# Differential attention scores: two 128-row passes a map replaced by three 64-row passes, both maps packed on the row halves

## The chip, the core and the metric

The kernel runs on one core of one Trainium2 chip. A core has five engines with instruction streams of their own: TensorE (PE: matmuls, with its weight loads shown apart as PEld), VectorE (DVE), ScalarE (ACT), GpSimd (POOL) and SyncE (SP, which here issues DMAs). Matmuls read SBUF, 128 partitions ("rows") wide, and write PSUM. The metric is the device time of the whole program in microseconds, as a median of several runs.

## The reference

One decoder layer on 1024 tokens of width 1024: RMSNorm, one input projection, an SSD (Mamba-2) mixer and a differential-attention mixer side by side, an output projection, and a SwiGLU feed-forward layer. The part that matters here is the attention, with 8 heads, each with two maps of head dimension 64 and one value of width 128:

```
q = q.reshape(bsz, seqlen, DA_HEADS, 2, DA_HEAD_DIM).transpose(3, 0, 2, 1, 4) * (DA_HEAD_DIM ** -0.5)
k = k.reshape(bsz, seqlen, DA_HEADS, 2, DA_HEAD_DIM).transpose(3, 0, 2, 1, 4)
...
s = jnp.einsum("mbhqd,mbhkd->mbhqk", qi, k).astype(f32)
p = jax.nn.softmax(jnp.where(mask, s, -jnp.inf), axis=-1)
w = p[0] - lam * p[1]
return jnp.einsum("bhqk,bhkv->bhqv", w.astype(v.dtype), v)
```

Each score is a sum over only 64 products. The mask is causal, and the queries go in 8 blocks of 128.

## The kernel before

Wide products are made in float32r. A float32 operand is split into a rounded part ("hi") and the rest ("lo", a second float32r number); `mm3` (L126 to L129) then forms hi·hi + hi·lo + lo·hi in three matmuls that sum up in one PSUM tile. Projections, output projection and feed-forward layer all use it. Values times weights (L611) and the transposes (L607, L624) are plain float32.

For a head, `qk` projects k and q of that head, each as 128 columns (64 of map 0, 64 of map 1) by 1024 tokens in two halves of 512. So the projected PSUM tile has map 0 on rows 0 to 63 and map 1 on rows 64 to 127. Its sinks (`sink_k`, L552 and L553; `sink_q`, L562 to L566) then lay out the operands of the scores so that a 128-row matmul covers two of the 64-product sums at once:

- `KS[:, m]` has the hi part of map m's keys on the map's own 64 rows and the lo part on the other 64 rows.
- `QH[:, m]` has the hi part of the queries on both halves of the rows, `QL[:, m]` the lo part on both.

Every instruction in these sinks works on 64 rows. ACT makes the hi parts (two instructions for k, two for q) and the second copy of QH (two); DVE makes the lo parts (two and two) and the second copy of QL (two).

`att_front(h, i)` makes the scores of head h and query block i. For map m it takes a two-bank PSUM tile `s` (pool `SC`, two buffers), and for each stretch `c` of up to 512 keys it runs two matmuls: QH against KS gives hi·hi + hi·lo (L585), QL against KS gives lo·hi + lo·lo (L586). Then DVE adds the mask (L587) and takes the row maximum (L588), ACT exponentiates and sums (L590), and DVE joins the two maps (L593 to L596). `att_back` of a block runs one step later: transposes (L607), a copy by ACT (L608), and the product with the values (L611). Block i has (i+1)·128 keys, so the score matmuls are 128, 256, 384 or 512 columns wide.

The program's order on each engine is not written out by hand in this stage: a scheduler builds it ahead of time from its own estimate of when operands and buffers are ready, and each engine then runs its list strictly in that order. In the attention it puts the matmuls of the next projections (`mm_q`, `mm_k`, `mm_v`) and of the output projection (`po_s`, `po_a`, L127 to L129) between the short steps of the attention, so that PE has work while DVE and ACT make the softmax. Only the feed-forward part has a PE order by hand.

Of the kernel before, what the change touches and what calls it, by code (L numbers as in the profile page):

```python
# [9 lines left out]
F32 = mybir.dt.float32  # L10
F32R = mybir.dt.float32r
AF = mybir.ActivationFunctionType
ALU = mybir.AluOpType
# [4 lines left out]
P = 128  # L18
# [6 lines left out]
def tile_hybrid_block(  # L25
# [68 lines left out]
    def norm_rows(parts, wbc, outs, name, pool=(), junk=None):  # L94
        """outs = RMSNorm of the row whose column pieces are parts; pieces in pool are weighted on Pool and scaled on ACT"""
        n, w = len(parts), DM // len(parts)
        ss = small.tile([P, n], F32, tag="ss1", name="ss_" + name)
        for i, p in enumerate(parts):
            nc.scalar.activation(outs[i] if junk is None else junk, p, AF.Square, accum_out=ss[:, i:i + 1])
        if n > 1:  # L100
            s1 = small.tile([P, 1], F32, tag="ss1", name="st_" + name)
            nc.vector.tensor_tensor(s1, ss[:, 0:1], ss[:, 1:2], op=ALU.add)
            ss = s1
        r = rstd_of(ss, DM, name)
        for i, (p, o) in enumerate(zip(parts, outs)):
            wi = wbc[:, i * w:i * w + w]
            if i in pool:
                nc.gpsimd.tensor_tensor(o, p, wi, op=ALU.mult)
                nc.scalar.mul(o, o, r)
            else:  # L110
                nc.vector.scalar_tensor_tensor(o, p, r, wi, op0=ALU.mult, op1=ALU.mult)
# [34 lines left out]
    def A4(shape, dt, name):  # L146
        return a4.tile(shape, dt, tag="a4", name=name)
# [15 lines left out]

# [1 line left out]
    def load_raw(src, shape, name):  # L165
# [14 lines left out]
    def z0_raw(a, u):  # L180
        """columns of dt and of the gate of group 0: 264 of 528"""
        raw = wp.tile([P, 4, 264], F32, tag="raw", bufs=2, name=f"wr_z0_{a}_{u}")
        k = slice(4 * u, 4 * u + 4)
        if a == 0:
            nc.sync.dma_start(raw[:, :, 0:16], w_in_k[:, k, C_DT:C_DT + 16])
            nc.sync.dma_start(raw[:, :, 16:264], w_in_k[:, k, C_Z:C_Z + 248])
        else:
            nc.sync.dma_start(raw, w_in_k[:, k, C_Z + 248:C_Z + 512])
        return raw
# [6 lines left out]

# [1 line left out]
    xs = []  # L198
# [16 lines left out]

# [1 line left out]
    prow = P4([69, P], F32, "prow")  # L217
# [17 lines left out]

# [1 line left out]
    def w_unit(src, shape, name, alloc=None):  # L237
# [10 lines left out]
    def proj_T(*jobs):  # L248
        """each job: a weight, a column, a name and sink(half, psum [128 columns, 512 tokens])"""
        us = [w_unit(w_k[:, :, col:col + P], [P, KD, P], name) for w_k, col, name, _ in jobs]  # L250
        for half in range(2):
            for (hi, lo), (_, _, name, sink) in zip(us, jobs):
                ps = MM([P, 512], f"mm_{name}_{half}")
                for k in range(KD):
                    mm3(ps, hi[:, k, :], lo[:, k, :], nhi[half][:, k, :], nlo[half][:, k, :], k == 0, k == KD - 1)
                sink(half, ps)

    def proj_z0(us, name, sink):
        """units of 264 columns; sink(t, psum [128 tokens, 264])"""
        for t in range(NT):  # L260
# [8 lines left out]
    def proj_nat(col, name, sink):  # L269
        """256 columns; sink(t, psum [128 tokens, 2 blocks from t, 256])"""  # L270
        us = [w_unit(w_in_k[:, 4 * u:4 * u + 4, col:col + 256], [P, 4, 256], f"{name}_{u}") for u in range(2)]
# [9 lines left out]

# [1 line left out]
    W16 = [P, NT, 16]  # L283
# [49 lines left out]

# [1 line left out]
    def conv_tiles(*tiles):  # L335
# [21 lines left out]
    def gate_dt():  # L357
        """the gate of group 0 and dt"""
        for a in range(2):
# [151 lines left out]

# [1 line left out]
    cneg = sp.tile([P, P], F32, tag="cs", name="cneg")  # L513
# [13 lines left out]
    def v_pair(hh):  # L527
        # [head][block] views of the two heads; in the last pair but one, the heads' tiles are freed one by one
        by_head = hh == NH // 2 - 2
# [13 lines left out]
    def qk(h):  # L543
        KS, QH, QL = [], [], []
        own = (slice(0, 64), slice(64, 128))

        def sink_k(half, ps):
            ks = A4([P, 2, 512], F32R, f"KS{h}_{half}")
            KS.append(ks)
            for m in range(2):  # L550
                a, b = own[m], own[1 - m]
                nc.scalar.copy(ks[a, m, :], ps[a, :])  # L552
                nc.vector.tensor_tensor(ks[b, m, :], ps[a, :], ks[a, m, :].bitcast(F32), op=ALU.subtract)  # L553

        def sink_q(half, ps):
            qh = A4([P, 2, 512], F32R, f"QH{h}_{half}")
            ql = (CV if h == NH - 1 and half == 0 else A4)([P, 2, 512], F32R, f"QL{h}_{half}")
            QH.append(qh)
            QL.append(ql)
            for m in range(2):  # L560
                a, b = own[m], own[1 - m]
                nc.scalar.mul(qh[a, m, :], ps[a, :], 0.125)  # L562
                nc.vector.scalar_tensor_tensor(ql[a, m, :], ps[a, :], 0.125, qh[a, m, :].bitcast(F32),
                                               op0=ALU.mult, op1=ALU.subtract)
                nc.scalar.copy(qh[b, m, :], qh[a, m, :].bitcast(F32))
                nc.vector.tensor_copy(ql[b, m, :], ql[a, m, :].bitcast(F32))  # L566
        jobs = ((w_in_k, C_K + h * P, f"k{h}", sink_k), (w_in_k, C_Q + h * P, f"q{h}", sink_q))
        for js in ([jobs] if h == NH - 1 else [[j] for j in jobs]):
            proj_T(*js)
        return KS, QH, QL  # L570

    def att_front(h, i, KS, QH, QL):
        n = f"{h}_{i}"
        Lk = (i + 1) * P
        qs = slice(i * P, (i + 1) * P)
        pm = []
        nmx = small.tile([P, 2], F32, tag="nmx", name="nmx" + n)
        sm = small.tile([P, 2], F32, tag="sm", name="sm" + n)
        for m in range(2):
            s = SC([P, T], f"s{n}_{m}")  # L580
            qr = slice((i % 4) * P, (i % 4) * P + P)
            for c in range(i // 4 + 1):
                w = min(Lk - c * 512, 512)
                sc = s[:, c * 512:c * 512 + w]
                nc.tensor.matmul(sc, QH[i // 4][:, m, qr], KS[c][:, m, :w], start=True, stop=False)  # L585
                nc.tensor.matmul(sc, QL[i // 4][:, m, qr], KS[c][:, m, :w], start=False, stop=True)  # L586
            nc.vector.tensor_tensor(s[:, qs], s[:, qs], cneg, op=ALU.add)  # L587
# [71 lines left out]

# [1 line left out]
    KG = 4  # L661
# [14 lines left out]
    def out_block(t, kys, ws, name, bank=MM):  # L676
        """two token blocks from t, 256 columns"""
        ps = bank([P, 2, 256], f"po_{name}_{t}")
# [47 lines left out]

# [1 line left out]
    # gate and up by Winograd's seven products: A are two column tiles by two halves of the contraction, B the two  # L728
    # halves of the contraction by two halves of the tokens; C = A B is summed up in PSUM (X, Y and Z)
    ORDER = (1, 2, 6, 5, 7, 3, 4)  # L730
# [4 lines left out]
    def room(p, early):  # L735
        """an operand B: [hi or lo][block of 128 rows] views of 512 tokens"""
        if early:
# [59 lines left out]
    def ffn_pair(pr, raws, order=ALL, ybank=SC):  # L797
        """silu(gate) * up of two column tiles; they and their sums as operands of the down projection to g_d"""
        sg, tm, c22, reg, sm = {}, {}, {}, [{}, {}], [{}, {}]
# [145 lines left out]
    def final_half(t, nh, last):  # L945
        """the first half of a row to be ready is weighted before its scale is known"""
        ho = h_parts(ho_all, t)
# [12 lines left out]

    # down, by the same seven products: A are the two halves of the tokens by two row tiles, B the row tiles by two
    # halves of the columns
    SLOT = {2: 0, 4: 1, 1: 2, 7: 3, 5: 4, 6: 5, 3: 6}
# [28 lines left out]
    for gi, prs in enumerate(groups):  # L992
# [5 lines left out]
        def psums(two, name):  # L998
            """four banks: one for each block of 128 tokens of a half"""
            if two:  # L1000
# [81 lines left out]
```

## Time and profile before

| | |
|---|---|
| runs, us | 1639.54, 1641.82, 1644.53 (median 1641.82) |
| profiled execution, span, us | 1643.3 (1.5 above the median of the runs) |
| granted TensorE clock | 0.995 |
| PE busy | 1597.2 us, 97%, 9170 matmuls |
| DVE, ACT, POOL busy | 1071.6 us, 775.8 us, 429.2 us |
| attention (first score matmul to the last blocks) | about 387 to 855 us |

The profiled execution's own time is its span; what lies outside it is not in the page. In the profile a matmul's duration runs from its start to a modelled end, and matmuls overlap in the array: the rate at which PE works is read from the distance between starts (about 0.23 us for 512 columns), not from the duration (about 0.39 us). A busy PE row is therefore no proof that PE is at its limit, and distances between starts are looked at beside it.

### The profile page before, as it was taken

What the parts mean: (1) busy time and instruction counts of PE and PEld (TensorE: products, weight loads), DVE (VectorE), ACT (ScalarE), POOL (GpSimd) and SP (SyncE); (2) the same over time, 40 slices, a digit from 0 to 9 for tenths busy, and PEclk for the clock granted to TensorE, in tenths of its full rate; (3) what the DMA queues carried; (4) which work ended last, traced back from release to release, by engine and by line L of the source; (5) the groups of instructions that cost most, each with busy time, mean ns of one, the idle gap of its engine ahead of it and who ended that gap; (6) DMA issues with size and microseconds to landing.
All of it is one profiled execution on the core that took longest, in us unless ns stands there. A gap on an engine that the chain in (4) does not pass through costs nothing. (4 is left out here: it accounts for less than half of the span.)

```text
span 1643.3 us, 23716 instructions
## 1 busy us (share of the span) xinstructions
PE 1597.2 (97%) x9170; PEld 1386.9 (84%) x9170; DVE 1071.6 (65%) x1682; ACT 775.8 (47%) x1608; POOL 429.2 (26%) x378
## 2 busy tenths in 40 slices
PE   6999999999999999999999998999999999999997
PEld 6988878887989989889999987888888888778885
DVE  5345745688776676677674477455555555898987
ACT  6444764456555565575552245333333333334445
POOL 4100330032000000013300034444444443542322
PEclk9999999999999999999999999999999999999999
DMA  5321451143011110147523221233333323944122
GB/s 195 110 79 52 129 163 56 36 142 92 24 46 39 46 33 27 45 130 229 162 77 116 84 99 56 96 102 104 111 116 118 98 96 134 365 166 186 39 103 103
DMA packets 105291, 172.78 MB, mean 105 GB/s; under 512 B 7813, under 2 KB 75530, under 8 KB 103770
## 3 DMA queue, kind: packets, MB, share of 16 engines
q1 hardware_dynamic: 95210, 137.11, 25.2%
q0 software_dynamic: 9968, 34.15, 6.3%
q8 instruction: 72, 1.18, 0.3%
q14 instruction: 41, 0.34, 0.1%
HBM read 125.82 MB, written 45.42 MB: 104 GB/s over the span
## 5 line engine op out<-in xcount | busy, mean ns | idle before, releaser
L127 PE MATMUL x<-n,wa 128*128 128x512 f32 x352 | 138.7, 396 | 0.0
L128 PE MATMUL x<-n,wa 128*128 128x512 f32 x352 | 138.7, 394 | 0.0
L129 PE MATMUL x<-n,wa 128*128 128x512 f32 x352 | 137.8, 394 | 0.0
L590 ACT ACTIVATE p<-s,nmx 128x256 f32<-128x256 f32 (+7 forms) x128 | 94.4, 740 | 53.2 <-DVE nmx L588 49.9
L172 ACT CAST wa<-s 128x512 fp32r<-128x512 f32 x88 | 54.7, 622 | 132.3 <-PE x L129 59.4
L173 DVE TENSOR_TENSOR wa<-s,wa 128x512 fp32r<-128x512 f32 x88 | 76.8, 873 | 51.1 <-ACT wa L172 50.8
L172 ACT CAST dg<-gd 128x512 fp32r<-128x512 f32 x77 | 47.7, 620 | 114.7 <-PE dx L129 57.2
L588 DVE TENSOR_REDUCE nmx<-s 128x1 f32<-128x256 f32 (+7 forms) x128 | 95.3, 754 | 2.4
L173 DVE TENSOR_TENSOR dg<-gd,dg 128x512 fp32r<-128x512 f32 x77 | 66.2, 862 | 23.3 <-ACT dg L172 23.2
L129 PEld LDWEIGHTS x<-n,wa 128*128 128x128 f32 x352 | 66.5, 189 | 15.1
L128 PEld LDWEIGHTS x<-n,wa 128*128 128x128 f32 x352 | 66.6, 189 | 14.8
L127 PEld LDWEIGHTS x<-n,wa 128*128 128x128 f32 x352 | 66.6, 189 | 14.8
L127 PE MATMUL mm_z<-wh_z,nhi 128*128 128x264 f32 (+1 forms) x256 | 75.9, 298 | 2.3 <-ACT wh_z L172 2.3
L611 PE MATMUL o<-v,p 128*128 128x128 f32 x576 | 77.7, 275 | 0.0
L129 PE MATMUL mm_z<-wh_z,nlo 128*128 128x264 f32 (+1 forms) x256 | 77.3, 303 | 0.0
L611 PEld LDWEIGHTS o<-v,p 128*128 128x128 f32 x576 | 73.5, 191 | 2.7
L128 PE MATMUL mm_z<-wl_z,nhi 128*128 128x264 f32 (+1 forms) x256 | 75.0, 294 | 0.0
L127 PE MATMUL mm_v<-wh_v,nhi 128*128 128x256 f32 x256 | 74.2, 290 | 0.0
L129 PE MATMUL mm_v<-wh_v,nlo 128*128 128x256 f32 x256 | 74.1, 290 | 0.0
L128 PE MATMUL mm_v<-wl_v,nhi 128*128 128x256 f32 x256 | 73.5, 287 | 0.0
L128 PE MATMUL po_a<-wl_wo,yh 128*128 128x256 f32 x256 | 72.6, 283 | 0.0
L91 POOL TENSOR_TENSOR rs_o<-ms_o,mhalf 128x4 f32<-128x4 f32 x16 | 18.0, 1125 | 208.4 <-DVE ms_o L89 208.3
(331 smaller groups left out, 5172.9 us busy)
## 6 DMA issues: line engine op xcount, KB each, us to landing
gd<-g_d SPq DMA_DIRECT2D x11, 1792.0 KB, 7.8
wr_g<-in_w_gate_dram SPq DMA_DIRECT2D x22, 512.0 KB, 3.8
wr_u<-in_w_up_dram SPq DMA_DIRECT2D x22, 512.0 KB, 4.3
g_d<-sg SPq DMA_DIRECT2D x22, 512.0 KB, 5.1
wr_d<-in_w_down_dram SPq DMA_DIRECT2D x22, 512.0 KB, 5.0
L<-cs_d POOLq DMA_DIRECT2D x16, 512.0 KB, 4.4
wr_y<-yT_d SPq DMA_DIRECT2D x16, 512.0 KB, 3.8
wr_wo<-in_w_out_dram SPq DMA_DIRECT2D x16, 512.0 KB, 3.5
```

Of the source, the lines that this page charges most:

```text
L91: nc.gpsimd.tensor_tensor(r, ms, mhalf[:, :w], op=ALU.pow)
L127: nc.tensor.matmul(ps, lh, rh, start=first, stop=False, skip_group_check=more)
L128: nc.tensor.matmul(ps, lh, rl, start=False, stop=False, skip_group_check=more)
L129: nc.tensor.matmul(ps, ll, rh, start=False, stop=last, skip_group_check=more)
L172: nc.scalar.copy(hi, raw)
L173: nc.vector.tensor_tensor(lo, raw, hi.bitcast(F32), op=ALU.subtract)
L588: nc.vector.reduce_max(nmx[:, m:m + 1], s[:, :Lk], axis=AX.X, negate=True)
L590: nc.scalar.activation(p[:, :Lk], s[:, :Lk], AF.Exp, bias=nmx[:, m:m + 1], accum_out=sm[:, m:m + 1])
L611: nc.tensor.matmul(o, wT[:, j * P:(j + 1) * P], vt[h % 2][j], start=(j == 0), stop=(j == i))
```

## The change

`KS` now has, on all 128 rows, the hi parts of both maps in slot 0 and the lo parts in slot 1; `QS` likewise for the queries. Each map keeps its own half of the rows, as it comes from the projection. So a sink is one ACT instruction and one DVE instruction on 128 rows in place of two and two (k) or four and four (q), and the tiles `QH` and `QL` become one tile `QS`.

For each stretch of keys and each map, `att_front` now runs three matmuls on 64 rows: hi·hi, hi·lo, lo·hi. lo·lo, which the 128-row form had in passing, is no longer computed. Map 0 uses rows 0 to 63, map 1 rows 64 to 127, and they write different PSUM tiles. The source names them in turn (map 0, map 1, map 0, ...), with both PSUM tiles taken ahead of the first matmul. The rest of the diff removes comments and docstrings.

```
     def qk(h):
-        KS, QH, QL = [], [], []
-        own = (slice(0, 64), slice(64, 128))
+        KS, QS = [], []
         def sink_k(half, ps):
             ks = A4([P, 2, 512], F32R, f"KS{h}_{half}")
             KS.append(ks)
-            for m in range(2):
-                a, b = own[m], own[1 - m]
-                nc.scalar.copy(ks[a, m, :], ps[a, :])
-                nc.vector.tensor_tensor(ks[b, m, :], ps[a, :], ks[a, m, :].bitcast(F32), op=ALU.subtract)
+            nc.scalar.copy(ks[:, 0, :], ps)
+            nc.vector.tensor_tensor(ks[:, 1, :], ps, ks[:, 0, :].bitcast(F32), op=ALU.subtract)
         def sink_q(half, ps):
-            qh = A4([P, 2, 512], F32R, f"QH{h}_{half}")
-            ql = (CV if h == NH - 1 and half == 0 else A4)([P, 2, 512], F32R, f"QL{h}_{half}")
-            QH.append(qh)
-            QL.append(ql)
-            for m in range(2):
-                a, b = own[m], own[1 - m]
-                nc.scalar.mul(qh[a, m, :], ps[a, :], 0.125)
-                nc.vector.scalar_tensor_tensor(ql[a, m, :], ps[a, :], 0.125, qh[a, m, :].bitcast(F32),
-                                               op0=ALU.mult, op1=ALU.subtract)
-                nc.scalar.copy(qh[b, m, :], qh[a, m, :].bitcast(F32))
-                nc.vector.tensor_copy(ql[b, m, :], ql[a, m, :].bitcast(F32))
+            qs = A4([P, 2, 512], F32R, f"QS{h}_{half}")
+            QS.append(qs)
+            nc.scalar.mul(qs[:, 0, :], ps, 0.125)
+            nc.vector.scalar_tensor_tensor(qs[:, 1, :], ps, 0.125, qs[:, 0, :].bitcast(F32),
+                                           op0=ALU.mult, op1=ALU.subtract)
...
-        for m in range(2):
-            s = SC([P, T], f"s{n}_{m}")
-            qr = slice((i % 4) * P, (i % 4) * P + P)
-            for c in range(i // 4 + 1):
-                w = min(Lk - c * 512, 512)
-                sc = s[:, c * 512:c * 512 + w]
-                nc.tensor.matmul(sc, QH[i // 4][:, m, qr], KS[c][:, m, :w], start=True, stop=False)
-                nc.tensor.matmul(sc, QL[i // 4][:, m, qr], KS[c][:, m, :w], start=False, stop=True)
+        ss = [SC([P, T], f"s{n}_{m}") for m in range(2)]
+        for c in range(i // 4 + 1):
+            w = min(Lk - c * 512, 512)
+            for j, (a, b) in enumerate(((0, 0), (0, 1), (1, 0))):
+                for m in range(2):
+                    o = slice(64 * m, 64 * m + 64)
+                    nc.tensor.matmul(ss[m][:, c * 512:c * 512 + w], QS[i // 4][o, a, qr], KS[c][o, b, :w],
+                                     start=j == 0, stop=j == 2)
+        for m, s in enumerate(ss):
             nc.vector.tensor_tensor(s[:, qs], s[:, qs], cneg, op=ALU.add)
```

The scheduler builds a new order for the whole attention. Three places show what it makes of the scores and the sinks. In the names, `s1_6_0` is the score tile of head 1, block 6, map 0; the number after the last underscore belongs to the buffer; `128x384` is the output, and `x3` means three such matmuls in a row.

PE, head 0, block 2 (384 keys), before:

```order
L129 MATMUL mm_q1_0_3821<-nhi0_134,wl_q1_3818 128x512
L585 MATMUL s0_2_0_3504<-KS0_0_3340,QH0_0_3406 128x384
L586 MATMUL s0_2_0_3504<-KS0_0_3340,QL0_0_3407 128x384
L585 MATMUL s0_2_1_3511<-KS0_0_3340,QH0_0_3406 128x384
L586 MATMUL s0_2_1_3511<-KS0_0_3340,QL0_0_3407 128x384
L127 MATMUL mm_q1_1_3856<-nhi1_135,wh_q1_3817 128x512
```

The same scores in the changed program, with the projection's matmuls between the two maps left out here but for the first and the last:

```order
L601 MATMUL wtp0_0_0_3481<-ident_69,p0_0_0_3445 128x128
L578 MATMUL s0_2_0_3490<-KS0_0_3340,QS0_0_3402 128x384 x3
L128 MATMUL mm_q1_1_3851<-nlo1_137,wh_q1_3819 128x512
...
L128 MATMUL mm_q1_1_3851<-nlo1_137,wh_q1_3819 128x512
L578 MATMUL s0_2_1_3491<-KS0_0_3340,QS0_0_3402 128x384 x3
L129 MATMUL mm_q1_1_3851<-nhi1_135,wl_q1_3820 128x512
```

The three 64-row matmuls of one map stand together, and thirteen 128-row matmuls of the projection stand between the maps.

PE, head 1, block 6 (512 and 384 keys), in the changed program:

```order
L605 MATMUL o0_4_4123<-v0_0_3095,p0_4_1_4058 128x128 x4
L578 MATMUL s1_6_0_4133<-KS1_0_3786,QS1_1_3876 128x512 x2
L578 MATMUL s1_6_1_4134<-KS1_0_3786,QS1_1_3876 128x512 x2
L578 MATMUL s1_6_0_4133<-KS1_0_3786,QS1_1_3876 128x512
L578 MATMUL s1_6_1_4134<-KS1_0_3786,QS1_1_3876 128x512
L578 MATMUL s1_6_0_4133<-KS1_1_3814,QS1_1_3876 128x384
L578 MATMUL s1_6_1_4134<-KS1_1_3814,QS1_1_3876 128x384
```

Here the maps do stand in turn. Over the whole program the 576 score matmuls stand in 136 unbroken stretches between 128-row matmuls, and of the 440 places inside a stretch where one score matmul follows another, 82 change the map and 358 stay with it.

ACT, the sink of the second half of q, head 4, before:

```order
L562 ACTIVATE QH4_1_5741<-mm_q4_1_5716 64x512
L565 CAST QH4_1_5741<-QH4_1_5741 64x512
L562 ACTIVATE QH4_1_5741<-mm_q4_1_5716 64x512
L613 ACTIVATE o3_0_5106<-o3_1_5161,r3_1_5124 128x128
L565 CAST QH4_1_5741<-QH4_1_5741 64x512
```

The same sink in the changed program, between a copy for head 3 and its softmax, is one instruction on 128 rows:

```order
L608 ACTIVATE p3_3_0_5192,sso3_0_5109<-o3_0_5108 128x128
L172 CAST wh_v3_0_6601<-wr_v3_0_6599 128x1024
L556 ACTIVATE QS4_1_5754<-mm_q4_1_5729 128x512
L584 ACTIVATE p3_5_1_5285,sm3_5_5264<-s3_5_1_5266,nmx3_5_5263 128x768
L602 COPY p3_4_1_5236<-wtp3_4_4_5298 128x128
```

The two copies and the second map's instruction are gone from this place.

The order of DMAs on SP is the same in both programs. On POOL's queue, the loads and stores of the output projection's first part stand about one head later.

More of the change, by code (lines that the diff above doesn't have):

```diff
@@ L569, in qk, with att_front @@
             proj_T(*js)
-        return KS, QH, QL
-    def att_front(h, i, KS, QH, QL):
+        return KS, QS
+    def att_front(h, i, KS, QS):
         n = f"{h}_{i}"
@@ L575, in att_front @@
         qs = slice(i * P, (i + 1) * P)
+        qr = slice((i % 4) * P, (i % 4) * P + P)
         pm = []
```

## The prediction, as put on record before the run

> **What bounds the kernel now.** I read the page first, then a table of stages, PE's waits, and PE in order of time inside the attention.
>
> ```profile
> PE 1597.2 (97%) x9170; PEld 1386.9 (84%) x9170; DVE 1071.6 (65%) x1682; ACT 775.8 (47%) x1608; POOL 429.2 (26%) x378
> PE   6999999999999999999999998999999999999997
> PEclk9999999999999999999999999999999999999999
> ```
>
> PE is busy in every slice at the same clock; ACT and DVE are not near their limit on the whole. A busy digit can hide a half-empty array, so the stage of the change needs its own look. The three stages below are what stands ahead of the scores, the attention, and the rest (us; busy per engine, in brackets instructions):
>
> ```profile
> core 0: us, PE busy (x) PEld busy (x) DVE busy (x) ACT busy (x) POOL busy (x), PEclk, DMA share, GB/s
> 0.00:387.00 387.00, 365.75 (x2212) 318.03 (x2213) 230.79 (x325) 211.86 (x396) 79.98 (x95) 0.99 0.34 106
> 387.00:855.00 468.00, 463.49 (x3133) 424.62 (x3133) 333.36 (x646) 275.97 (x678) 56.39 (x73) 1.00 0.26 80
> 855.00:1643.30 788.30, 768.00 (x3829) 644.28 (x3827) 507.45 (x713) 288.00 (x534) 292.80 (x211) 0.99 0.34 120
> ```
>
> In the attention PE lacks 4.5 of 468 us, DVE has 135 us free and ACT 192. PE's waits from 370 to 855 us, all of them (total, times, longest):
>
> ```profile
> PE s L585 <- ACT p L590: 2.9, 3, 1.7
> PE wtp L607 <- ACT o L613: 1.2, 2, 0.8
> PE mm_k L127 <- DVE QL L563: 1.1, 1, 1.1
> PE po_s L127 <- DVE QL L563: 0.4, 1, 0.4
> PE yp L471 <- DVE y L480: 0.3, 1, 0.3
> ```
>
> That is 5.9 us. So nothing but PE sets the end of this stage: its work comes from queued projections whenever the softmax is not ready. Time taken off or put on PE here goes straight to the end.
>
> **What the scores cost PE now.** Count and widths:
>
> ```profile
> L585 PE MATMUL s<-KS,QH 128*128 128x512 f32 x96 | 39.4, 410 | 2.9 <-ACT p L590 2.9
> L586 PE MATMUL s<-KS,QL 128*128 128x512 f32 x96 | 38.1, 397 | 0.0
> L585 PE MATMUL s<-KS,QH 128*128 128x384 f32 x32 | 11.4, 355 | 0.0
> L586 PE MATMUL s<-KS,QL 128*128 128x384 f32 x32 | 11.0, 344 | 0.0
> L585 PE MATMUL s<-KS,QH 128*128 128x256 f32 x32 | 9.2, 290 | 0.0
> L586 PE MATMUL s<-KS,QL 128*128 128x256 f32 x32 | 8.9, 281 | 0.0
> L586 PE MATMUL s<-KS,QL 128*128 128x128 f32 x32 | 8.7, 275 | 0.0
> L585 PE MATMUL s<-KS,QH 128*128 128x128 f32 x32 | 7.3, 230 | 0.0
> ```
>
> The mean durations overlap each other, so I price a matmul by the distance to the next start (first column of the order in time, three places):
>
> ```profile
> 398.68 0.33 PE L585 MATMUL s<-KS,QH 128*128 128x384 f32 x1
> 398.85 0.34 PE L586 MATMUL s<-KS,QL 128*128 128x384 f32 x1
> 399.03 0.34 PE L585 MATMUL s<-KS,QH 128*128 128x384 f32 x1
> ...
> 412.92 0.22 PE L585 MATMUL s<-KS,QH 128*128 128x128 f32 x1
> 412.98 0.28 PE L586 MATMUL s<-KS,QL 128*128 128x128 f32 x1
> 413.09 0.33 PE L128 MATMUL mm_v<-wl_v,nhi 128*128 128x256 f32 x1
> ...
> 416.55 0.39 PE L585 MATMUL s<-KS,QH 128*128 128x512 f32 x1
> 416.78 0.39 PE L586 MATMUL s<-KS,QL 128*128 128x512 f32 x1
> 417.01 0.28 PE L585 MATMUL s<-KS,QH 128*128 128x256 f32 x1
> 417.13 0.28 PE L586 MATMUL s<-KS,QL 128*128 128x256 f32 x1
> ```
>
> 512 columns take 0.23 us, 384 take 0.175, 256 take 0.12. The two of 128 take 0.06 and 0.11: under so short a matmul the next weights are not in place in time, and the second pays 0.05 more; mean 0.085. Sum: 192 x 0.23 + 64 x 0.175 + 64 x 0.12 + 64 x 0.085 = 44.2 + 11.2 + 7.7 + 5.4 = **68.5 us**.
>
> **The change, part by part.**
>
> *Three passes for two.* The columns streamed by a matmul are the keys; that only 64 rows carry data makes none of them shorter. 576 in place of 384, in the same mix of widths, are 102.8 us if each waits for the one ahead: **+34.3 us**.
>
> *What the two halves save by running side by side.* Two matmuls on different rows and in different PSUM tiles may share the array; the trace has no such pair. The bound below is nothing. For the bound above only neighbours count, since PE takes its list in order, and the built order, unlike the source, rarely alternates: of 440 places where one score matmul follows another, 82 change the map (28 between 512-wide ones, 19 of 384, 10 of 256, 14 of 128, 11 between unequal widths). If each hid the narrower of the two, that is 28 x 0.23 + 19 x 0.175 + 10 x 0.12 + 14 x 0.085 + some 1.2 = 13.4 us. But in a chain map 0, map 1, map 0 the third waits for the first, since both need the same rows. Walking through the 136 stretches with this rule (a matmul starts once its predecessor has started and its own rows are free) leaves **-8.5 us**, which I take. Reason: different rows and different tiles leave nothing in the program to hold the second back.
>
> *Going over from 128-row to 64-row matmuls and back.* 136 stretches are 272 such changes, and none in the program before. Bound below: nothing. Bound above: nothing of the next kind starts until the last matmul is out (recorded 0.39 less 0.23 of distance, 0.16), and its weights are loaded after that (0.11, the distance that follows the second 128-wide matmul): 0.27 us each, 73 us. The nearest row is that pair of 128-wide matmuls, where weights that came late cost 0.05: **+13.6 us**.
>
> The Trainium skill, "TensorEngine Tiling (Array Packing)", section "Tiling Modes", says that changing the tiling mode, unlike changing the tile, drains the engine. No run here shows it yet; by it the full 0.16 is paid, which is the first rival below.
>
> *The sinks.*
>
> ```profile
> L552 ACT CAST KS<-mm_k 64x512 fp32r<-64x512 f32 x32 | 18.5, 578 | 13.8 <-DVE KS L553 11.0 <-PE mm_k L129 2.5
> L562 ACT ACTIVATE QH<-mm_q 64x512 fp32r<-64x512 f32 x32 | 18.9, 590 | 7.8 <-DVE QL L563 5.3 <-PE mm_q L129 2.2
> L565 ACT CAST QH<-QH 64x512 fp32r<-64x512 f32 x32 | 19.8, 618 | 0.9
> L553 DVE TENSOR_TENSOR KS<-mm_k,KS 64x512 fp32r<-64x512 f32 x32 | 22.0, 689 | 4.5 <-ACT KS L552 3.5
> L563 DVE SCALAR_TENSOR_TENSOR QL<-mm_q,QH 64x512 fp32r<-64x512 f32 x32 | 21.9, 686 | 2.5 <-ACT QH L562 1.6 <-PE s L585 0.5
> L566 DVE CAST QL<-QL 64x512 fp32r<-64x512 f32 x32 | 13.7, 427 | 1.0
> L838 ACT COPY tm<-x 128x512 f32<-128x512 f32 x22 | 12.8, 583 | 9.9 <-PE x L129 9.9
> L840 DVE COPY tm<-x 128x512 f32<-128x512 f32 x22 | 15.1, 688 | 14.7 <-PE x L129 13.8 <-DMA g_d<-sg 0.9
> ```
>
> The last two rows show that 128 rows of 512 out of PSUM cost what 64 rows cost. So of ACT's 57.2 us remain 32 x 0.585 = 18.7, of DVE's 57.6 remain 32 x 0.688 = 22.0: 38.5 and 35.6 us less. Both engines are covered by PE, so this is worth no more than PE's waits, 5.9 us: the two on QL (1.5) surely go, the three on the softmax (2.9) in part, since a longer score stage and a lighter ACT both give the softmax time. I take **-3 us** (bounds 0 and -5.9). If PE had not covered them, the stage would have been up to 36 us shorter; that cover is what makes the trade poor. The waiting that is late next is DVE's and ACT's own, for scores, and nobody on the path waits for those.
>
> *Order.* DMAs on SP keep their order. The output projection's first part moves one head later as filler; at the end of the attention its next part (`po_a`) is still there to fill PE, as before, so I count nothing. Should one head's end lack filler, a wait like the longest above, 1.7 us, is the price.
>
> **Sum.** 1643.3 (the profiled span) + 34.3 - 8.5 + 13.6 - 3.0 = 1679.7; the profiled execution lay 1.5 above the median of the runs, so **1678 us**, 2.2% slower. With its terms at their bounds but the drain not paid in full, from 1643.3 + 34.3 - 13.4 + 0 - 5.9 - 1.5 = 1657 to 1643.3 + 34.3 + 27 (0.1 per change) - 1.5 = 1703.
>
> **The rivals.**
>
> *Each change of kind pays the whole drain.* 272 x 0.16 = 43.5 in place of 13.6: **1708 us**; with the weights' 0.11 on top, 1738. For it: the new weights sit in another shape of the array. Against it: no row of this trace shows PE emptying between two kinds of matmul.
>
> *Weights cannot be loaded under a matmul on the same rows.* Then each of the 358 places that stay with a map pays up to 0.11, 39.4 us, in place of the 13.6: 1643.3 + 34.3 - 8.5 + 39.4 - 3 - 1.5 = **1704 us**. Against it: at 128 rows the loads are hidden under 512-wide matmuls that hold the same rows (0.23 from start to start, each with its own weights). The skill's page "TensorE: Matmul & The Clock Gate", section "Part 3: Packing small matmuls — row/col tiling", says that weight loads overlap running matmuls only where the row group differs; the distances above contradict it for 128-row matmuls, and nothing here shows it for 64-row ones.
>
> *Faster: the halves always run side by side.* If PE starts a map's three matmuls beside the other map's whatever stands between, 102.8 us become 51.4, 17.1 less than now, and with the waits 1643.3 - 17.1 - 3 - 1.5 = **1622 us**. It decides from 34.3 us of overlap on, two thirds of the largest possible; neighbours allow 13.4. For it only the source's order, which the built order does not keep.
>
> *No difference.* Overlap and vanished waits would have to give 13.4 + 5.9 and the changes of kind nothing; 15 us are still missing. Only if PE had idle room that the distances do not show.
>
> **How the numbers follow.** Forecast 0.58; drain 0.23; weights 0.12; faster 0.04; no difference 0.03. The range reaches from the forecast's low end past both middle rivals, but not to drain and load together: 1657 to 1726. A difference of 0.3% (5 us) is about what the runs can tell from none; slower 0.93, same 0.03, faster 0.04.
>
> **What would show it.** In the changed profile the score rows have 576 matmuls; starts of 512-wide ones of one map should stand 0.23 apart (0.34 speaks for the weights), of two maps in turn almost together (0.23 speaks against any overlap). From the last score matmul to the next 128-row one and from the last 128-row one to the first score, the distance should be about 0.05 over the plain one; 0.16 or more is the drain. The attention should end some 36 us later, with PE still full, and everything behind it should be as long as before; ACT's and DVE's busy times should fall by 38 and 36 us. I am wrong in kind if the attention does not grow, and wrong in size by the terms for overlap and changes, which no row of before carries.

## The result and the profile after

| | before | changed |
|---|---|---|
| median of 4 runs, us | 1642.34 (1639.54 to 1644.53) | 1707.45 (1705.40 to 1709.55) |
| ratio, 95% interval | | 1.0393 (1.0373 to 1.0413) |
| profiled span, us | 1643.3 | 1705.3 |
| score matmuls | 384 | 576 |

The change makes the kernel 3.9% slower. The forecast was 1678 with a range of 1657 to 1726: the sign and the range hold, but the loss is 65 us where 36 were forecast. The two profiled spans differ by 62 us: a span is 1.8 us shorter than the time of its run, and the profiled execution before was some 3 us slower than the median of its runs (1643.3 + 1.8 against 1642.3). What follows accounts for the 62.

The page of the changed kernel, busy time of the engines and PE and its clock in 40 slices:

```profile
PE 1667.6 (98%) x9362; PEld 1408.6 (83%) x9362; DVE 1038.6 (61%) x1618; ACT 741.0 (43%) x1544; POOL 427.1 (25%) x378
PE   6999999999999999999999999999999999999997
PEclk9999999999999999999999999999999999999999
```

PE is as full as before and its clock is the same, so the 62 us between the spans are no idle time. DVE and ACT lost 33 and 35 us of work, nearly what the lighter sinks promised. DVE's own rows by shape confirm the price put on them:

```profile
L557 DVE SCALAR_TENSOR_TENSOR QS<-mm_q,QS 128x512 fp32r<-128x512 f32 x16 | 11.0, 687 | 10.4 <-ACT QS L556 10.4
L551 DVE TENSOR_TENSOR KS<-mm_k,KS 128x512 fp32r<-128x512 f32 x16 | 10.9, 684 | 0.3 <-ACT KS L550 0.3
```

128 rows take 0.69 us, as 64 rows did, and there are half as many instructions (ACT's take 0.58 and 0.60 us). PE sets the end of the stage, so beyond the few us of waits that PE loses, none of this can reach the end of the program. The table by stage (ahead of the scores, attention, rest; busy us per engine):

```profile
0.00:385.00 385.00, 365.46 (x2213) 318.53 (x2213) 227.29 (x318) 207.53 (x389) 79.94 (x95) 0.99 0.34 107
385.00:893.00 508.00, 508.00 (x3112) 419.53 (x3111) 290.22 (x571) 237.55 (x613) 54.77 (x72) 1.00 0.21 67
893.00:1705.30 812.30, 794.14 (x4041) 670.55 (x4039) 521.10 (x729) 295.92 (x543) 292.40 (x211) 0.99 0.34 120
```

The attention takes 508 us in place of 468, and PE is counted busy in all of it; between 370 and 895 us the view of waits has no PE row left, where it had 5.9 us before. The last stage is 24 us longer only because 212 matmuls more fall into it (4041 for 3829): part of the output projection that used to fill PE during the attention now runs behind it. The loss itself is made in the attention.

A busy PE hides how it was made. The order in time of PE in the changed kernel (start, duration) at one stretch of three 512-wide score matmuls:

```profile
406.50 0.28 PE L128 MATMUL mm_v<-wl_v,nhi 128*128 128x256 f32 x1
406.62 0.28 PE L129 MATMUL mm_v<-wh_v,nlo 128*128 128x256 f32 x1
406.83 0.96 PE L578 MATMUL s<-KS,QS 64*128 64x512 f32 x3
407.71 0.39 PE L127 MATMUL mm_v<-wh_v,nhi 128*128 128x256 f32 x1
407.94 0.28 PE L128 MATMUL mm_v<-wl_v,nhi 128*128 128x256 f32 x1
408.06 0.28 PE L129 MATMUL mm_v<-wh_v,nlo 128*128 128x256 f32 x1
```

A 256-wide matmul is followed after 0.12 us (406.50 to 406.62, 407.94 to 408.06). Going into the scores it takes 0.21 (406.62 to 406.83). The three scores take 0.88 us to the next start, where 3 x 0.23 are 0.69, and the first 256-wide matmul after them needs 0.23 in place of 0.12. That is 0.09 + 0.19 + 0.11 = 0.39 us on top for one stretch, 0.2 for each change between 128-row and 64-row matmuls. The weight loads at the same place:

```profile
406.50 0.19 PEld L129 LDWEIGHTS mm_v<-wh_v,nlo 128*128 128x128 f32 x1
406.62 0.28 PE L129 MATMUL mm_v<-wh_v,nlo 128*128 128x256 f32 x1
406.82 0.53 PEld L578 LDWEIGHTS s<-KS,QS 64*128 64x128 f32 x3
406.83 0.96 PE L578 MATMUL s<-KS,QS 64*128 64x512 f32 x3
407.71 0.19 PEld L127 LDWEIGHTS mm_v<-wh_v,nhi 128*128 128x128 f32 x1 [0.36 <-issue]
407.71 0.39 PE L127 MATMUL mm_v<-wh_v,nhi 128*128 128x256 f32 x1
```

The load of L129 starts 0.12 us ahead of its matmul, under the one before. At the change, both ways, the load starts with its matmul (0.01 us and nothing ahead): it was not made under the matmuls of the other kind.

The same over the whole program: for each matmul the distance to the next start, less the plain distance for its width (0.231, 0.175, 0.119 and 0.086 us for 512, 384, 256 and 128 columns, 0.122 for 264, 0.112 for a pass of plain float32). This is a sum over the records of the two traces:

```
us                                           before  changed
plain time of the score matmuls                68.7    103.0
saved where two of them run side by side       -         -13.8
on top inside and around their stretches        6.2     53.2
on top everywhere else, waits included         47.3     42.1
```

The 53.2 are 13.3 on the way in, 13.2 behind the first score matmul, 13.75 on the way out and 12.95 behind the first matmul after it: four times about 0.1 us at 136 stretches. The size of the last row depends on the prices taken for the many other matmuls; only its change counts here. The differences, +34.3 - 13.8 + 47.0 - 5.2, are 62.3 us; the spans differ by 62.0, since the first matmul of the changed program starts 0.3 us earlier.

### The profile page after: what moved, and what is told of

Read it like the earlier page. It is cut to its first block, busy times and chain, and to the rows that moved or that the text cites. A ratio compares the mean times of both kernels' runs of the same rounds, so it can differ in the third digit from the quotient of the medians.

```text
span 1705.3 us, 23974 instructions
## 1 busy us (share of the span) xinstructions
PE 1667.6 (98%) x9362; PEld 1408.6 (83%) x9362; DVE 1038.6 (61%) x1618; ACT 741.0 (43%) x1544; POOL 427.1 (25%) x378
## 5 line engine op out<-in xcount | busy, mean ns | idle before, releaser
L129 PE MATMUL x<-n,wa 128*128 128x512 f32 x352 | 138.0, 395 | 0.0
L578 PE MATMUL s<-KS,QS 64*128 64x512 f32 (+3 forms) x576 | 125.7, 369 | 0.0
L581 DVE TENSOR_TENSOR s<-s,cneg 128x128 f32<-128x128 f32 x128 | 36.7, 297 | 116.3 <-PE s L578 115.7
L578 PEld LDWEIGHTS s<-KS,QS 64*128 64x128 f32 x576 | 78.9, 184 | 31.7 <-issue 11.8
L129 PEld LDWEIGHTS x<-n,wa 128*128 128x128 f32 x352 | 66.7, 189 | 15.2
L129 PE MATMUL mm_z<-wh_z,nlo 128*128 128x264 f32 (+1 forms) x256 | 77.3, 303 | 0.0
L607 ACT ACTIVATE o<-o,r 128x128 f32<-128x128 f32 x64 | 23.4, 366 | 122.6 <-PE o L605 122.4
L129 PE MATMUL mm_v<-wh_v,nlo 128*128 128x256 f32 x256 | 75.5, 295 | 0.0
```

The costliest lines, as they stand in the source:

```text
L129: nc.tensor.matmul(ps, ll, rh, start=False, stop=last, skip_group_check=more)
L578: nc.tensor.matmul(ss[m][:, c * 512:c * 512 + w], QS[i // 4][o, a, qr], KS[c][o, b, :w], start=j == 0, stop=j == 2)
L607: nc.scalar.mul(oa[:, i % 4, :], o, r[:, 0:1])
```

## The experiments

The theory after the result: a change between 128-row and 64-row matmuls costs 0.2 us, whatever the width. The expectations of the second to the fourth run still put it at 0.15, from a first count of 41 us over 272 changes. The rivals: the third pass costs more than its streaming time; the weights of a map are not loaded while that map's rows are in use; PE keeps to its list even where the other half of the rows is free.

### Three passes without a change of kind

The three passes are made by 128-row matmuls; `QS` gets a tile for each map, with zeros on the other map's rows, so that nothing changes kind. The sinks of q then work on 64 rows again, as before the change:

```diff
+                nc.gpsimd.memset(qz[m][b, :, :].bitcast(F32), 0.0)
-                    o = slice(64 * m, 64 * m + 64)
-                    nc.tensor.matmul(..., QS[i // 4][o, a, qr], KS[c][o, b, :w], ...)
+                    nc.tensor.matmul(..., QS[i // 4][m][:, a, qr], KS[c][:, b, :w], ...)
```

> Three passes for each map as in the change, but each on all 128 rows: the queries stand in a tile for each map with zeros on the other map's rows, so no matmul is on 64 rows and PE never changes its kind. If the changes between 128-row and 64-row matmuls carry what the forecast missed (41 us in the trace of the change), this one has the third pass alone: 1642.3 + 34.3, less some 3 for waits = 1674. If three passes themselves, or weights that come late, cost more than their columns, it comes out near the change: 1700 or more.

Measured: 1682.68 us (1680.56 to 1684.42), ratio 1.0242 (1.0227 to 1.0257). The place in this kernel that answers to the stretch shown above, and PE's waits from 370 to 895 us:

```profile
407.94 0.28 PE L127 MATMUL mm_v<-wh_v,nhi 128*128 128x256 f32 x1
408.06 0.85 PE L580 MATMUL s<-KS,QS 128*128 128x512 f32 x3
408.75 0.28 PE L128 MATMUL mm_v<-wl_v,nhi 128*128 128x256 f32 x1
408.87 0.28 PE L129 MATMUL mm_v<-wh_v,nlo 128*128 128x256 f32 x1
```

```profile
PE s L580 <- ACT p L586: 5.8, 2, 5.4
PE yp L471 <- DVE y L480: 1.1, 1, 1.1
```

Here 0.12 us lead into the three scores, they take 0.69, and 0.12 follow: nothing on top. The third pass costs its streaming time, +34.3, and the rest up to the 37.7 us between the spans is about the one wait of 5.4 us on the softmax, less what vanished of the old waits. The 9 us above the 1674 expected are about this wait and the 3 us of waits that I had counted as gone. The same three passes are 24.8 us cheaper here, without any two of them side by side, than in the changed kernel, which does run some side by side (-13.8). So the halves cost more than they save.

### The maps one after the other in one stretch

The scores of a block are kept together: on PE their order is written out, all of map 1 and then all of map 0, and the first one waits until both score tiles are free:

```diff
+        with tc.manual_schedule(engines={mybir.EngineType.PE}):
+            for m in (1, 0):
+                for c in range(i // 4 + 1):
+                    for j, (a, b) in enumerate(((0, 0), (0, 1), (1, 0))):
+                        mm = nc.tensor.matmul(...)
+                        if last_exp: tc.add_manual_dep(mm.ins, last_exp.pop().ins.name, ...)
```

> The change with the 64-row matmuls of a block kept in one stretch, map 1's first, then map 0's, the first of them once both score tiles are free: 78 stretches (156 changes of kind) in place of 136 (272), and the maps follow each other in 56 places only. If a change of kind costs about 0.15 each: 1642.3 + 34.3 - 8.8 of overlap + 156 x 0.15 (23) - 5 of waits = 1686. If the missing time belongs to each 64-row matmul (41 us over 576, 0.07 each) and not to the changes: 1642.3 + 34.3 - 8.8 + 41 - 5 = 1704.

Measured: 1675.61 us, ratio 1.0203 (1.0187 to 1.0219). Better than both expectations, and the reason is a surprise. Two places in order of time on PE, the first in this kernel, the second in the changed one:

```profile
410.74 0.28 PE L129 MATMUL mm_v<-wh_v,nlo 128*128 128x256 f32 x1
410.94 0.97 PE L581 MATMUL s<-KS,QS 64*128 64x512 f32 x6
411.84 0.39 PE L127 MATMUL mm_v<-wh_v,nhi 128*128 128x256 f32 x1
```

```profile
436.27 0.28 PE L129 MATMUL mm_v<-wh_v,nlo 128*128 128x256 f32 x1
436.48 0.96 PE L578 MATMUL s<-KS,QS 64*128 64x512 f32 x3
437.38 0.44 PE L601 MATMUL wtp<-ident,p 128*128 128x128 f32 x2
437.74 0.96 PE L578 MATMUL s<-KS,QS 64*128 64x512 f32 x3
```

Six 512-wide matmuls take 0.90 us from the first start to what follows (410.94 to 411.84), and so do three (436.48 to 437.38), although in this kernel only one place of the six changes the map. The single records show why. A row of the view gives a group; these are the starts of a stretch of twelve in it, in ns from the first, with the map worked out from the place in the list:

```
list:    map 1: 512 512 512 256 256 256   map 0: 512 512 512 256 256 256
started: map 1   0  344  577  809  927 1046
         map 0  584  919 1149 1385 1501 1614
```

The seventh of the list starts 7 ns after the third, ahead of three matmuls that stand before it in the list and wait for map 1's rows. PE does not keep to its list where a queued matmul needs only the free half of the rows. So what is said ahead of the prediction, that each engine runs its list strictly in order, does not hold for these matmuls. The reach is short: map 0's half was free from the first start on, but the seventh, then six places on, started only with the third, four places on, and it did so in each stretch of twelve of this kind. Over the program 28.4 us are saved by this; a walk strictly in the order of the list would save 8.8. The first matmul on each half is followed on that half only after 0.34 us, every later one after 0.23: the weights of the same half are loaded under a running matmul, all but the second ones of a stretch.

### The maps in turn

The same with the loop over the maps innermost: 75 stretches, every second matmul on the other half.

```diff
+            for c in range(i // 4 + 1):
+                for j, (a, b) in enumerate(((0, 0), (0, 1), (1, 0))):
+                    for m in (1, 0):
```

> As the run with the maps apart, with the two maps' matmuls in turn: 75 stretches (150 changes of kind), 501 places that change the map and none that stays. If two 64-row matmuls on different rows really run side by side over their whole length, the 102.8 us of columns shrink to 52.4: 1642.3 - 16.4 + 150 x 0.15 (22.5) - 5 = 1643, some 42 us below the run with the maps apart. If the pairs only start together but share the array's rate, it equals that run: 1686. If each 64-row matmul costs 0.07 more and changes cost nothing: 1642.3 - 16.4 + 41 - 5 = 1662.

Measured: 1665.42 us, ratio 1.0140 (1.0126 to 1.0155). The row of the 512-wide score matmuls, of the kernel with the maps apart and of this one (busy us, mean ns of one; busy time counts a moment once, however many run in it):

```profile
L581 PE MATMUL s<-KS,QS 64*128 64x512 f32 x288 | 65.5, 420 | 0.7 <-ACT p L590 0.7
```

```profile
L581 PE MATMUL s<-KS,QS 64*128 64x512 f32 x288 | 44.8, 422 | 2.7 <-ACT p L590 2.7
```

The same 288 matmuls, each as long as before, fit into 44.8 us in place of 65.5: now all run in pairs. The saving is 50.7 us of 103.0, half of the plain time. It is still slower than before by 23 us of span, and 22 us above the 1643 of one expectation. The third pass less the overlap gives back 16.4 (34.3 - 50.7); the 150 changes add about 26 to what stood around the scores before, and some 14 are more idling and delay of PE, about half of it by name in its waits (13.4 us in all, 5.9 before; 5.1 on the score tiles, 6.1 on inputs of the output projection). PE's waits from 370 to 895 us, and PE's row of the window 600 to 700 us:

```profile
PE s L581 <- ACT p L590: 5.1, 6, 1.9
PE po_a L127 <- DVE hx L698: 3.7, 1, 3.7
PE po_s L127 <- DVE hx L698: 1.9, 2, 1.1
PE wtp L608 <- DVE p L597: 1.4, 1, 1.4
PE o L612 <- ACT p L609: 0.8, 2, 0.4
...
600.00:700.00 100.00, 94.77 (x648) 81.11 (x647) 57.09 (x114) 48.59 (x127) 5.46 (x7) 0.98 0.12 38
```

A stretch here waits for both score tiles at once, and PE lacks 5 of 100 us. So this run shows the full overlap, but not its price free of waits.

### Two blocks in one stretch

To pay fewer changes with no wait on both tiles, the blocks with up to 512 keys take one two-bank tile for both maps, and two such blocks are scored in one stretch, 12 matmuls; larger blocks as in the run before. 56 stretches.

```diff
+        if i < 4:
+            if i % 2 == 0:
+                pair = [SC([P, 2, 512], f"s{h}_{i + d}") for d in range(2)]
+                scores(KS, QS, [(i + d, [pair[d][:, m, :] for m in range(2)]) for d in range(2)])
+        else:
+            ss = [SC([P, T], f"s{n}_{m}") for m in range(2)]
+            scores(KS, QS, [(i, ss)])
```

> As the run with the maps in turn, with the first four blocks of a head taken two at a time (both maps of a block in one score tile): 56 stretches, 112 changes of kind. At 0.15 for each: 1642.3 - 16.9 + 112 x 0.15 (17) - 5 = 1637, below the kernel before. If the changes are free and the cost is in the 64-row matmuls: 1662. If the softmax now starts too late for PE's other work to fill in, waits of PE on the scores' buffers grow beyond the 5.9 us of before, and it stays above 1643.

Measured: 1645.87 us, ratio 1.0023 (1.0012 to 1.0035). PE's waits in the attention, the 512-wide scores, and the window 600 to 700 us:

```profile
PE otp L642 <- DVE r L611: 2.1, 1, 2.1
PE s L577 <- ACT p L607: 0.6, 2, 0.3
...
L577 PE MATMUL s<-KS,QS 64*128 64x512 f32 x288 | 44.2, 416 | 0.6 <-ACT p L607 0.6
...
600.00:700.00 100.00, 99.89 (x689) 86.50 (x687) 57.91 (x117) 49.68 (x127) 4.87 (x6) 1.00 0.11 35
```

The waits of the run before are gone and PE is full again. Counted as above: 103.0 plain, 50.5 saved, 22.3 on top at 112 changes (0.2 each), 46.9 elsewhere. Scores and changes together are 74.8 us against 74.9 before (68.7 + 6.2): full overlap and so few stretches only pay back what the third pass and the changes cost. The time lies 9 us above the 1637 and 16 below the 1662 that were expected. It stays above 1643, as the third expectation said, but not for its reason: PE's waits are 2.7 us, less than the 5.9 before.

### The maps by three

This is the direct test of the order. Only the two inner loops are swapped: three matmuls of map 1, then three of map 0, and so on; the stretches stay.

```diff
-                    for j, (a, b) in enumerate(((0, 0), (0, 1), (1, 0))):
-                        for m in (1, 0):
+                    for m in (1, 0):
+                        for j, (a, b) in enumerate(((0, 0), (0, 1), (1, 0))):
```

> As the run with two blocks, but the three matmuls of one map stand together, then the three of the other, for each stretch of keys (54 stretches). If PE runs a matmul on the free half of the rows ahead of up to three queued ones that wait for the busy half, as the starts in the run with the maps apart suggest, this costs what the run with two blocks costs: 1646, within 3. If it takes matmuls in the program's order and only neighbours overlap, the scores' columns take 77 us in place of 52: 1646 + 25 = 1671.

Measured: 1646.51 us, ratio 1.0017 (1.0005 to 1.0030), no different from the run with two blocks, and 24 us below the value for a PE that keeps to its list.

```profile
L577 PE MATMUL s<-KS,QS 64*128 64x512 f32 x288 | 44.8, 415 | 0.6 <-ACT p L607 0.6
```

44.8 us of busy time against 44.2 above: PE pairs the matmuls by itself. The single records say the same: in the stretch of twelve at 412.90 us the first six start 0, 10, 341, 351, 581 and 591 ns from the first, so the fourth of the list starts with the first. The Trainium skill, page "TensorE: Matmul & The Clock Gate", section "Part 3: Packing small matmuls — row/col tiling", says that matmuls start and end strictly in program order. The starts here contradict it for matmuls on different halves of the rows; the ends are modelled, and show nothing on that part.

### More changes, nothing else

Ahead of the second stretch of keys of the larger blocks stands one small 128-row matmul into columns that the scores then overwrite. It cuts stretches in two, 85 in place of 56, and leaves the scores alone.

```diff
+                    if c:
+                        nc.tensor.matmul(ss[1][:, 512:576], ident, ident[:, :64], start=True, stop=True)
```

> As the run with two blocks, with one small 128-row matmul (64 columns, its result is overwritten) between the scores of the first 512 keys and those behind them, in the blocks that have both: 85 stretches in place of 56, 58 more changes of kind, the same 64-row matmuls. If a change costs 0.2: 1646 + 58 x 0.2 (12) + 32 x 0.11 for the added matmuls (4) = 1662. If the cost sits in the 64-row matmuls: 1646 + 4 = 1650.

Measured: 1664.91 us, ratio 1.0128 (1.0102 to 1.0154), 19.0 us above the run with two blocks for 58 changes more, and 15 above the 1650 for a cost that sits in the 64-row matmuls. One place in order of time on PE:

```profile
412.11 0.41 PE L579 MATMUL s<-KS,QS 64*128 64x512 f32 x2
412.45 0.43 PE L575 MATMUL s<-ident 128*128 128x64 f32 x2
412.82 0.44 PE L579 MATMUL s<-KS,QS 64*128 64x128 f32 x4
```

The added matmul is plain float32 and shows as two passes, where the expectation counted one. Both take 0.37 us from their start to the next (412.45 to 412.82), where two plain ones take 0.22. By distances, 18 us are at the stretches and the added matmuls, 6 elsewhere (of these, a wait of 4.0 us of the output projection); the profiled execution of this run was 3 us slower than its median. If the 64 short passes cost the plain 0.112 each, 7 of the 18 us are theirs, and 11 are left for 58 changes, 0.19 each. That split is worked out, not measured apart, but the price agrees with the 0.2 from the other runs.

### The copies of q by DMA

What the lighter sinks are worth by themselves: the kernel before, its two same-engine copies of q replaced by DMAs.

```diff
-                nc.scalar.copy(qh[b, m, :], qh[a, m, :].bitcast(F32))
-                nc.vector.tensor_copy(ql[b, m, :], ql[a, m, :].bitcast(F32))
+                nc.gpsimd.dma_start(qh[b, m, :], qh[a, m, :])
+                nc.gpsimd.dma_start(ql[b, m, :], ql[a, m, :])
```

> The kernel before, with the second copies of the queries' parts (32 ACT and 32 DVE instructions, 33.5 us of busy time together) moved by DMAs that POOL issues. If the lighter sinks are worth no more than PE's waits on them (1.5 us, with some of the 4.1 on the softmax), it is 1637 to 1642, no difference that can be told. If the sinks were worth more than the waits show, 1635 or less; if the DMAs come late, above 1645.

Measured: 1651.13 us, ratio 1.0052 (1.0032 to 1.0072). PE's waits from 370 to 895 us:

```profile
PE otp L624 <- DVE o L618: 4.2, 2, 3.0
PE s L585 <- ACT p L590: 4.1, 5, 1.5
...
PE po_s L127 <- DVE QL L563: 0.2, 1, 0.2
```

The waits on QL are nearly gone, from 1.5 to 0.2 us, but the time is past the 1645 that stood for late DMAs, since waits on the softmax and behind it grew by more, though ACT and DVE had less to do (757.7 and 1059.1 us for 775.8 and 1071.6 over the program). The built order is a different one, and whether it or the DMAs' own time makes the new waits is not told apart here. So less work on the engines under PE's cover bought nothing in this build; what it would be worth without the DMAs and in the old order is not shown.

## Why the prediction was right in sign and wrong in size

- **What bounds the stage.** Right: PE alone sets its end. The changed kernel's attention has no PE wait at all, and 62 us more of PE time are 62 us more of span.
- **Three passes, +34.3.** Right. The run with three 128-row passes has the plain distances and comes out at +37.7 us of span with 6.9 us of waits of PE, 5.4 of them one wait on the softmax.
- **Overlap, -8.5 (bounds 0 and -13.4).** Measured -13.8, just outside the bound. The step that failed is "only neighbours count, since PE takes its list in order": a score matmul on the free half starts ahead of up to three queued ones. In the changed kernel this could give little: in 110 of the 136 stretches there no two matmuls start together, and most of these hold three matmuls of one map; in kernels with whole blocks in a stretch it gives the full half.
- **Changes of kind, 272 x 0.05 = +13.6.** This is the term that was mis-sized: it measured 53.2 us, 0.196 each, and +47.0 against what stood around the scores before. I took the nearest row, a late weight load of 0.05, and said that no row spoke for more; a 64-row matmul ahead of or behind 128-row ones was not in the trace, so the row was near in form only. The bound of 0.27 held. The rival that a change pays the drain was right in kind: 0.09 us at the change itself, and then 0.105 before the second matmul of the new kind. That second part fits a weight load that could start only with the first matmul, as its record does, so that the next load comes late; the first part is less than the 0.16 that I put on a full drain. That rival's time, 1708, is the measured one by luck: its price a change, 0.16, is below the 0.196 measured, and the overlap and the waits, which it took from the forecast, gave back 7.5 us more. The Trainium skill, page "TensorEngine Tiling (Array Packing)", section "Tiling Modes", says that changing the mode drains the engine. The trace agrees in part: each change has its pause, but the first score matmul starts at 406.83, ahead of the recorded (modelled) end of the one before, 406.62 + 0.28 = 406.90, so a wait for the full drain is not shown. What makes the 0.09 stays open; that it comes with the change is shown.
- **Weights not loadable on the same rows.** Wrong as a rival: inside a stretch the matmuls of one map stand 0.231 us apart. Only the second of a stretch is late, which is part of the change.
- **Waits and sinks, -3 (bounds 0 and -5.9).** Measured -5.2 for everything away from the scores. All of PE's old waits went, since a PE with more to do leaves the softmax more time.
- **Faster, chance 0.04.** Its premise, that PE starts a map's matmuls beside the other map's whatever stands between, is half true: other score matmuls may stand between, up to four places on; across the projection's 128-row matmuls no pair formed. It could not have won even so. With all of it true the run with two blocks just breaks even.

Put together: 34.3 - 13.8 + 47.0 - 5.2 in place of 34.3 - 8.5 + 13.6 - 3.0. Of the 26 us that are missing in the forecast, the changes of kind are +33 and the other two terms -7.5.

## What to carry to other kernels

Count the places where PE goes between full-height and half-height matmuls before counting the rows saved: here each costs 0.2 us on PE, both ways and at nearly every width, and none of it shows as idle time. Three 64-row passes side by side in place of two 128-row ones save a quarter of the old time and pay two changes a stretch, 0.4 us, so a stretch pays only if its old matmuls took more than 1.6 us together; the largest block here takes 8 x 0.231 = 1.85 us in four PSUM banks, the others, and the pairs of small ones in the run with two blocks, 1.62 or less. That no version of this split wins here is argued from these prices; the best one run came out 0.2% slower than before.

## What the hardware did that I had not expected

- PE takes matmuls out of the order of its list where they use the free half of the rows: the seventh of a stretch started 7 ns after the third, and swapping the loops over maps and parts moved the time by 0.6 us of 1646.
- Two 64-row matmuls on different halves each keep their full pace. In pairs whose starts lie mostly 3 to 10 ns apart, 288 of them 512 wide are busy for 44.2 us against 82.9 us for as many of 128 rows in a row:

```profile
L580 PE MATMUL s<-KS,QS 128*128 128x512 f32 x288 | 82.9, 403 | 0.5 <-ACT p L586 0.3
```

- The record of a matmul's duration grows at a change as well: the first 256-wide matmul behind the scores is recorded at 0.39 us (at 407.71), the ones after it at 0.28.
